# Starting the attention of the first 512 queries after 6 instead of 20 pieces of the in-projection's last part, two pieces per step

## Chip, cores and metric

The kernel runs on one core of one Trainium2 chip. The metric is the device time of one execution in microseconds (us). Three runs of the kernel before gave a median of 2692.12 us (2691.47 to 2698.45).

## The reference

One layer of a hybrid encoder block on 2048 frames of width 1024, in f32. The part that matters here is the stick-breaking attention, 8 heads of width 64, in blocks of 128 queries, strictly causal:

```
z = einsum('bhqd,bhkd->bhqk', qb, kb) * d**-0.5
mask = s_pos[None, :] < t_pos[:, None]
log_one_minus = where(mask, log_sigmoid(-z), 0.0)
between = cumsum(shifted log_one_minus, reverse)      # over later keys
weights = where(mask, exp(log_sigmoid(z) + between), 0.0)
out = einsum('bhqk,bhkd->bhqd', weights, vb)
```

Ahead of it stand the modulated RMSNorm and one in-projection, `proj = h @ w_in`, whose columns are q, k and v of the attention and the inputs of a gated linear attention (GLA). Behind it stand the out-projection, a second norm, the up-projection with a causal convolution and a gate, the down-projection, and a final norm.

## The kernel before

Every f32 matmul against weights is done as three matmuls of rounded parts (high by high, high by low, low by high). The 2048 frames are worked in four chunks of 512, numbered 0 to 3. The in-projection goes over the weight blocks in an order fixed by hand, and stores q, k and v of each chunk in HBM (`q_hi`, `q_lo`, `k_hl`, `v_hl`). In its second half the GLA of the last chunks runs between the matmuls. It ends with the GLA's last tile: four transposes (L467), the split into `mh` and `ml` on ScalarE and VectorE (L470), and their stores `mg_hi` and `mg_lo` (L473) on SyncE's queue (SP).

What then is left of the in-projection is written as a generator, `last_pieces` (L771): v of chunk 3 in four row tiles (L779 to L781, weights against `hh` and `hl`) and the last two heads of k of chunk 3 (L789 to L791). It yields after each **piece**, three matmuls of 128x128 by 512 columns; there are 4 x 8 + 8 = 40 pieces. A finished row tile is split by ScalarE and VectorE into `vt`, of which there is one buffer (L783, L784), and stored (L785).

The attention is a loop of **steps** (L1097): step n takes 128 queries against 512 keys of one head. Its parts are `score` (L981, L982 and on the diagonal the mask, L984), `weigh` (two sigmoids on ScalarE, L1000 and L1001; a scan on VectorE, L1006; a product on GpSimd, L1008), six steps later `turned` (PE transposes, L70, and the split into `ah` and `al`, L129 and L130), and two more steps later `value` (L1033, L1034). Four steps are a unit: one head, one chunk of queries, one chunk of keys. The first 512 queries are steps 0 to 31, and within a unit the widths are 128, 256, 384 and 512 keys. `fetch` (L958) issues the loads of a unit on SP: q (L964), `kt` (L967) and `vt` (L969), six steps ahead; the first two units' are issued before the loop.

The order of PE's matmuls inside the loop is the order in which they are written (`in_order`, L1096). Other engines' instructions and SP's loads are put in an order by a scheduler when the program is built, and each engine and SP then works through its own queue strictly in order. The pieces are woven into the loop by a credit:

```
work, rate, credit, tail = last_pieces(), FR, 0.0, []
for _ in range(PRE):
    next(work)
for u in range((FA + 3) // 4):
    fetch(u)
...
    for n in range(last_step):
        ...
        credit += rate
        while credit >= 1.0:
            credit -= 1.0
            if work is not None and next(work, True):
                work = None
```

`PRE` pieces run before step 0, and `FR` pieces at the end of each step until none is left; the step after that opens the pools of the out-projection (L1102) and begins to load its weights, 1 MB at every sixth step (L1106, `wo`). Whatever the two numbers are, the out-projection of the first chunk is woven in from step 63 on (L1128, L1131). Steps without pieces or out-projection are called **unfilled** here.

Of the kernel before, what the change touches and what calls it, by code (L numbers as in the profile page):

```python
# [32 lines left out]
LATE = 2  # L33
GROUPS = ((0,),(1,),(2,3),(4,5),(6,7))
CUTS = (0,4,8)
PRE = 20
WI = 6
ST = 24
FR = 1.0
FA = 6  # L40
ADA = ((2,2,2,2,1,1,1,1,1,0,1),(1,1,1,1,1,1,0,0,0,0,0))
PREP = ((0,0,0,0,1,0,1,0,1,0,1),(1,0,1,0,1,1,0,0,0,0,0))
# [5 lines left out]
def hybrid_block(ctx, tc, x, c, w_ada, b_ada, g1, w_in, w_fg2, b_fg2, g_gla, w_out, g2,  # L48
# [722 lines left out]
    def last_pieces():  # L771

        hh, hl = hs[3]
        for tt in range(4):
            sl = slice(tt * P, (tt + 1) * P)
            ps = ps_mm.tile([P, CH], F, name="mm")
            for k in range(KD):
                wh, wl = w_v[k]
                pe.matmul(out=ps, lhsT=hh[:, k, sl], rhs=wh, start=k == 0, stop=False)  # L779
                pe.matmul(out=ps, lhsT=hh[:, k, sl], rhs=wl, start=False, stop=False)  # L780
                pe.matmul(out=ps, lhsT=hl[:, k, sl], rhs=wh, start=False, stop=k == KD - 1)  # L781
                yield
            vt = ev.tile([P, H, 2, HD], R, name="vt", bufs=1)  # L783
            split_from_psum(vt[:, :, 0, :], vt[:, :, 1, :], ps.rearrange("p (h d) -> p h d", h=H))  # L784
            dma.dma_start(out=v_hl[3][tt * P:(tt + 1) * P], in_=f32(vt.rearrange("p h a d -> p h (a d)")))  # L785
        ps = ps_mm.tile([P, CH], F, name="mm")
        for k in range(KD):
            wh, wl = w_k[k]
            pe.matmul(out=ps, lhsT=wh, rhs=hh[:, k], start=k == 0, stop=False)  # L789
            pe.matmul(out=ps, lhsT=wh, rhs=hl[:, k], start=False, stop=False)  # L790
            pe.matmul(out=ps, lhsT=wl, rhs=hh[:, k], start=False, stop=k == KD - 1)  # L791
            yield
        eh = ev_tile("eh", R)
        el = ev_tile("el", R)
        split_from_psum(eh, el, ps)
        for a in range(2):
            dma.dma_start(out=k_hl[3][6 + a, 0:64, :], in_=f32(eh[a * 64:(a + 1) * 64]))
            dma.dma_start(out=k_hl[3][6 + a, 64:128, :], in_=f32(el[a * 64:(a + 1) * 64]))
# [289 lines left out]
    last_step = N + LEAD + LATE  # L1088
    work, rate, credit, tail = last_pieces(), FR, 0.0, []
    open_at, start = None, -1  # L1090
    for _ in range(PRE):
        next(work)
# [545 lines left out]
```

## Time and profile before

| | us |
|---|---|
| median of three runs | 2692.12 |
| the profiled execution, its own time | 2685.92 |
| its span, first to last instruction | 2684.2 |
| PE busy (94% of the span) | 2521.2 |
| VectorE busy (68%) | 1831.4 |
| ScalarE busy (49%) | 1306.4 |
| GpSimd busy (48%) | 1289.3 |
| mean granted clock of PE, share of full speed | 0.987 |

Engines: PE is TensorE, PEld its weight loads, DVE VectorE, ACT ScalarE, POOL GpSimd, SPq SyncE's DMA queue. A row of a timeline gives start, duration, engine, line, operation, output<-input and shapes; brackets at its end hold the idle time of the engine just before it and what ended that. Successive matmuls overlap: one of 512 columns is listed with 0.39 us, but the next one starts 0.23 us later. A row of windows gives the stretch, its length, the busy time of PE, PEld, DVE, ACT and POOL (instructions in brackets), the granted PE clock (1.00 is 2.4 GHz, 0.50 is 1.2 GHz), the mean busy share of the 16 DMA engines, and GB/s. A row of waits gives the waiting instruction, its releaser, the total, how often, and the longest. A row of DMA issues gives the count, the size and the time from issue to landing.

### The profile page before, as it was taken

The page shows a single profiled execution, that of the slowest core. Times are in us where ns is not written, and L with a number is a line of the kernel's source. Part 1 is how long each engine was busy: PE and PEld are TensorE (multiplying, and loading weights), DVE is VectorE, ACT ScalarE, POOL GpSimd, SP SyncE. Part 2 cuts the span into 40 slices and gives each one's busy share as a digit, 9 for nine tenths or more (in the row PEclk, how much of TensorE's full clock was granted, in tenths as well). Part 3 has the DMA queues.
Part 4 walks back from the last instruction along what each step waited for, and adds up shares of the span by engine and source line. Part 5 has one row for each costly group of instructions (what it writes and reads, how often), then busy time and mean ns, then how long its engine had stood idle before and what let it go on. Part 6 is the DMA issues. An engine that isn't in the chain of part 4 may idle for free. (4 is left out here: it accounts for less than half of the span.)

```text
span 2684.2 us, 36445 instructions
## 1 busy us (share of the span) xinstructions
PE 2521.2 (94%) x12118; PEld 2060.4 (77%) x12118; DVE 1831.4 (68%) x2511; ACT 1306.4 (49%) x2328; POOL 1289.3 (48%) x1094
## 2 busy tenths in 40 slices
PE   5999999999899999999889999989999999999996
PEld 5788788888677777777777777767877877888885
DVE  6535652254988999998567767788777777454668
ACT  4523234233877888887444444454444444333343
POOL 2202131121755556766655645576566563252446
PEclk9999999999999999999999999999999999999998
DMA  8657954586865444554633443455445447544572
GB/s 284 193 170 253 288 169 144 154 250 183 260 184 172 131 140 146 165 161 131 220 114 114 138 138 102 132 186 169 147 137 173 146 146 252 166 142 128 167 271 79
DMA packets 406827, 459.06 MB, mean 171 GB/s; under 512 B 35806, under 2 KB 271596, under 8 KB 404592
## 3 DMA queue, kind: packets, MB, share of 16 engines
q1 hardware_dynamic: 406640, 456.74, 53.9%
q8 instruction: 96, 1.57, 0.2%
q14 instruction: 91, 0.75, 0.1%
HBM read 313.51 MB, written 143.13 MB: 170 GB/s over the span
## 5 line engine op out<-in xcount | busy, mean ns | idle before, releaser
L1008 POOL TENSOR_TENSOR bt<-bt,om 128x512 f32<-128x512 f32 (+2 forms) x320 | 314.5, 988 | 220.3 <-DVE om L1006 122.9
L1185 POOL TENSOR_TENSOR wub<-ring,wub 128x512 fp32r<-128x512 f32 x176 | 236.5, 1356 | 264.8 <-ACT wub L1184 264.4
L1231 PE MATMUL v<-h,wua 128*128 128x512 f32 x1056 | 259.7, 395 | 7.8 <-DVE halo L1297 5.4
L1231 PE MATMUL v<-h,wub 128*128 128x512 f32 x1056 | 250.2, 393 | 12.5 <-DVE v L1235 6.5
L1231 PE MATMUL g<-h,wub 128*128 128x512 f32 x1056 | 257.9, 390 | 1.5 <-DVE g L1235 1.5
L1006 DVE TENSOR_TENSOR_SCAN om<-sg,om,zero 128x513 f32<-128x513 f32 x189 | 240.6, 1273 | 16.0 <-ACT sg L1000 14.8
L1231 PEld LDWEIGHTS v<-h,wub 128*128 128x128 f32 x1056 | 199.8, 190 | 56.4 <-ACT wub L1184 6.4
L1231 PEld LDWEIGHTS v<-h,wua 128*128 128x128 f32 x1056 | 199.1, 189 | 55.4 <-ACT wua L1184 5.4
L1185 POOL TENSOR_TENSOR wua<-ring,wua 128x512 fp32r<-128x512 f32 x132 | 195.1, 1481 | 77.7 <-ACT wua L1184 73.3
L1231 PEld LDWEIGHTS g<-h,wub 128*128 128x128 f32 x1056 | 198.2, 188 | 43.7 <-DVE g L1235 1.9
L1180 DVE TENSOR_TENSOR ring<-ring 128x512 f32<-128x512 f32 x176 | 172.5, 999 | 85.4 <-DMA ring<-in_w_up_dram 61.7
L1604 PE MATMUL d<-h,wub 128*128 128x512 f32 x924 | 222.9, 391 | 0.0
L70 PE MATMUL tr<-ident,bt 128*128 128x128 f32 x1120 | 179.9, 277 | 37.5 <-DVE al L130 25.0
L1362 POOL TENSOR_TENSOR h<-h,h 128x512 fp32r<-128x512 f32 x77 | 116.6, 1518 | 193.0 <-ACT h L1361 176.5
L130 DVE TENSOR_TENSOR al<-tr,ah 128x512 fp32r<-128x512 f32 (+1 forms) x320 | 193.0, 603 | 19.5 <-ACT ah L129 18.7
L1604 PEld LDWEIGHTS d<-h,wub 128*128 128x128 f32 x924 | 173.5, 188 | 37.6
L286 POOL TENSOR_TENSOR wr<-wst,wr 128x1024 fp32r<-128x1024 f32 x28 | 69.4, 2484 | 276.2 <-ACT wr L285 276.2
L129 ACT ACTIVATE ah<-tr 128x512 fp32r<-128x512 f32 (+1 forms) x320 | 179.4, 561 | 25.9 <-PE tr L70 25.3
L70 PEld LDWEIGHTS tr<-ident,bt 128*128 128x128 f32 x1120 | 126.6, 140 | 84.6 <-DVE al L130 35.8
L1001 ACT ACTIVATE bt<-z 128x512 f32<-128x512 f32 (+2 forms) x320 | 173.6, 543 | 0.0
L1184 ACT ACTIVATE wub<-ring 128x512 fp32r<-128x512 f32 x176 | 107.8, 625 | 134.4 <-DVE ring L1180 83.9
L400 PE MATMUL mm<-wr,hh 128*128 128x512 f32 (+1 forms) x448 | 169.5, 378 | 2.9 <-DVE vt L130 2.2
(309 smaller groups left out, 6067.6 us busy)
## 6 DMA issues: line engine op xcount, KB each, us to landing
ring<-in_w_up_dram SPq DMA_DIRECT2D x176, 256.0 KB, 3.9
ring<-hid_s SPq DMA_DIRECT2D x154, 256.0 KB, 4.1
wst<-in_w_in_dram SPq DMA_DIRECT2D x45, 512.0 KB, 7.6
hid_s<-cval SPq DMA_DIRECT2D x88, 256.0 KB, 2.3
kt<-k_hl SPq DMA_DIRECT2D x80, 256.0 KB, 3.0
vt<-v_hl SPq DMA_DIRECT2D x80, 256.0 KB, 3.3
hid_s<-ring SPq DMA_DIRECT2D x66, 256.0 KB, 2.7
ast<-in_w_ada_dram SPq DMA_DIRECT2D x32, 512.0 KB, 5.5
```

The source lines that it names most:

```text
L70: pe.transpose(out=o, in_=i, identity=ident)
L129: act.activation(out=hi, in_=ps, func=AF.Copy)
L130: dve.tensor_tensor(out=lo, in0=ps, in1=f32(hi), op=ALU.subtract)
L400: pe.matmul(out=ps[:, :n], lhsT=hh[:, k, sl], rhs=wh, start=k == 0, stop=False)
L1001: act.activation(out=b1, in_=z[:, :w], func=AF.Sigmoid, scale=0.125)
L1006: dve.tensor_tensor_scan(out=om[:, 0:n_][:, ::-1], data0=beta[:, 0:n_][:, ::-1], data1=zero[0][:, 0:1].broadcast_to([P, n_]), initial=firs ...
L1008: pool.tensor_tensor(out=b1, in0=b1, in1=om[:, 1:w + 1], op=ALU.mult)
L1180: dve.tensor_tensor(out=t_, in0=a, in1=b, op=op)
L1185: eng.tensor_tensor(out=t_[:, 1], in0=src, in1=f32(t_[:, 0]), op=ALU.subtract)
L1231: pe.matmul(out=ps, lhsT=lhsT, rhs=rhs, start=begin and k == 0 and m == 0, stop=k == KH - 1 and m == 2, skip_group_check=not begin)
L1362: pin(eng.tensor_tensor(out=t_[:, 1], in0=src, in1=f32(t_[:, 0]), op=ALU.subtract))
L1604: pin(pe.matmul(out=ps, lhsT=hd[:, l_, tsl], rhs=w[:, r_], start=begin and q == 0 and m == 0, stop=q == NQ2 - 1 and m == 2, skip_group_che ...
```

## The change

Two constants are changed: the loop begins after 6 pieces, and each step takes two pieces instead of one.

```
-PRE = 20
+PRE = 6
 WI = 6
 ST = 24
-FR = 1.0
+FR = 2.0
```

PE's order ahead of step 0. `tp` transposes belong to the GLA's last tile, `mm` matmuls to pieces, and `z` is a step's score. Before, the end of the 20 pieces:

```order
L779 MATMUL mm<-wr,hh 128x512
L780 MATMUL mm<-wr,hh 128x512
L781 MATMUL mm<-wr,hl 128x512
L981 MATMUL z<-kt,qh 128x256
L982 MATMUL z<-kt,ql 128x256
L984 LDWEIGHTS identb
L984 MATMUL z<-mask,identb 128x128
L779 MATMUL mm<-wr,hh 128x512
```

In the change, from the GLA's last transposes on:

```order
L70 MATMUL tp<-ident,sq 128x128 x4
L779 MATMUL mm<-wr,hh 128x512
L780 MATMUL mm<-wr,hh 128x512
L781 MATMUL mm<-wr,hl 128x512
L779 MATMUL mm<-wr,hh 128x512
L780 MATMUL mm<-wr,hh 128x512
L781 MATMUL mm<-wr,hl 128x512
L981 MATMUL z<-kt,qh 128x256
L982 MATMUL z<-kt,ql 128x256
L984 LDWEIGHTS identb
L984 MATMUL z<-mask,identb 128x128
L779 MATMUL mm<-wr,hh 128x512
```

Up to the sixth piece PE's order is the same in both; the first score has moved ahead of the 14 pieces that stood before it.

SP's queue at the same place (`mg_hi` and `mg_lo` are the GLA's last stores, the first `kt` and `vt` are unit 0's, `v_hl_75<-vt` stores a row tile of the pieces):

```order
 L967 DMA kt<-k_hl_68 128x512
 L969 DMA vt<-v_hl_72 128x4x128
-L785 DMA v_hl_75<-vt 128x1024
 L967 DMA kt<-k_hl_68 128x512
 L969 DMA vt<-v_hl_72 128x4x128
```

The first row here is directly behind the store of `mg_lo` in both programs; a row tile's store has moved from between the loads of units 0 and 1 to a place behind the first loads of `kt` and `vt`.

PE's order where the pieces end, in the change, from the last piece (step 16) into step 18 (`tr` are the attention's transposes, `av` its values):

```order
L789 MATMUL mm<-hh,wr 128x512
L790 MATMUL mm<-hl,wr 128x512
L791 MATMUL mm<-hh,wr 128x512
L981 MATMUL z<-kt,qh 128x256
L982 MATMUL z<-kt,ql 128x256
L984 LDWEIGHTS identb
L984 MATMUL z<-mask,identb 128x128
L70 MATMUL tr<-ident,bt 128x128 x2
L1033 MATMUL av<-ah,vt 128x384
L1034 MATMUL av<-al,vt 128x384
L981 MATMUL z<-kt,qh 128x384
L982 MATMUL z<-kt,ql 128x384
```

Steps 17, 18 and 19 have one piece each before and none in the change.

## Rows read from the trace of the kernel before

**Rows 1.** The page, its first part: busy time of each engine
```profile
PE 2521.2 (94%) x12118; PEld 2060.4 (77%) x12118; DVE 1831.4 (68%) x2511; ACT 1306.4 (49%) x2328; POOL 1289.3 (48%) x1094
```

**Rows 2.** Windows: busy time of each engine before, in and after the unfilled stretch
```profile
core 0: us, PE busy (x) PEld busy (x) DVE busy (x) ACT busy (x) POOL busy (x), PEclk, DMA share, GB/s
650.83:691.38 40.55, 40.39 (x228) 32.77 (x226) 27.80 (x61) 24.91 (x62) 18.13 (x24) 1.00 0.68 209
691.38:757.00 65.62, 52.39 (x322) 39.52 (x321) 65.21 (x120) 58.72 (x138) 48.49 (x51) 1.00 0.99 295
780.00:800.00 20.00, 20.00 (x112) 16.58 (x111) 14.42 (x25) 12.78 (x28) 10.40 (x12) 1.00 0.53 163
```

**Rows 3.** Waits of PE from 691 to 757 us (total, times, longest)
```profile
PE tr L70 <- DVE al L130: 8.3, 16, 1.2
```

**Rows 4.** Timeline of PE around step 0
```profile
650.60 0.39 PE L781 MATMUL mm<-wr,hl 128*128 128x512 f32 x1
650.83 0.39 PE L779 MATMUL mm<-wr,hh 128*128 128x512 f32 x1
...
660.35 0.28 PE L981 MATMUL z<-kt,qh 128*128 128x256 f32 x1
```

**Rows 5.** Timeline of SP's queue: the loads that step 0 needs, a later load
```profile
650.98 0.36 SPq L473 DMA_DIRECT2D mg_lo<-ml  x1
651.44 0.49 SPq L967 DMA_DIRECT2D kt<-k_hl  x1
653.73 0.36 SPq L969 DMA_DIRECT2D vt<-v_hl  x1
...
700.43 0.58 SPq L967 DMA_DIRECT2D kt<-k_hl  x1
```

**Rows 6.** Timeline of PE: the score that waited for the later load
```profile
703.62 0.36 PE L981 MATMUL z<-kt,qh 128*128 128x256 f32 x1 [0.59 <-DMA kt<-k_hl]
```

**Rows 7.** Windows: DMA traffic after the first load
```profile
654.00:654.25 0.25, 0.25 (x3) 0.20 (x2) 0.00 (x0) 0.00 (x0) 0.00 (x0) 1.00 0.22 74
654.25:654.50 0.25, 0.25 (x3) 0.21 (x2) 0.00 (x0) 0.00 (x0) 0.00 (x0) 1.00 0.00 0
```

**Rows 8.** DMA issues from 654.6 to 654.9 us: the second load
```profile
kt<-k_hl SPq DMA_DIRECT2D x1, 256.0 KB, 5.0
```

**Rows 9.** Timeline of PE: gaps elsewhere in the kernel
```profile
111.13 0.48 PE L70 MATMUL tp<-ident,gfr 128*65 128x128 f32 x1 [2.41 <-DVE gfr L521]
...
383.33 0.30 PE L70 MATMUL tp<-ident,xt 128*128 128x128 f32 x1 [4.26 <-DVE ms L123]
...
1361.56 0.47 PE L1231 MATMUL v<-h,wub 128*128 128x512 f32 x1 [2.41 <-DVE v L1235]
...
1808.52 7.92 PE L1231 MATMUL v<-h,wub 128*128 128x512 f32 x22 [6.01 <-ACT wub L1184]
```

**Rows 10.** Windows: the granted clock behind those gaps
```profile
111.00:116.00 5.00, 4.87 (x15) 3.91 (x16) 4.96 (x4) 0.00 (x0) 2.21 (x1) 0.66 0.14 24
383.00:389.00 6.00, 5.67 (x34) 5.70 (x35) 2.15 (x8) 3.52 (x8) 1.66 (x3) 0.72 0.69 240
1361.00:1364.00 3.00, 2.44 (x11) 2.04 (x12) 2.04 (x4) 1.75 (x3) 2.92 (x3) 1.00 0.47 135
1808.52:1815.00 6.48, 6.48 (x17) 5.09 (x18) 6.48 (x7) 1.54 (x3) 3.55 (x4) 0.56 0.21 78
```

**Rows 11.** Timeline of PE: first instruction of steps 17, 20, 21, 24 and 25
```profile
686.20 0.28 PE L981 MATMUL z<-kt,qh 128*128 128x256 f32 x1
...
691.38 0.28 PE L981 MATMUL z<-kt,qh 128*128 128x256 f32 x1
...
692.38 0.28 PE L981 MATMUL z<-kt,qh 128*128 128x256 f32 x1
...
696.73 0.28 PE L981 MATMUL z<-kt,qh 128*128 128x256 f32 x1
...
697.96 0.28 PE L981 MATMUL z<-kt,qh 128*128 128x256 f32 x1
```
## The prediction

> **What bounds the kernel now.** The page comes first: PE is busy for 94% of the span and no other engine for more than 68% [rows 1]. So the question is where PE idles, and whether the change makes it idle more or less. I then took the windows around the pieces [rows 2]. From 650.83 us, behind the sixth piece, to 691.38, the start of step 20 and so the end of the pieces, PE is busy for 40.39 of 40.55 us: PE is the limit there, and DVE has 40.55 - 27.80 = 12.75 us to spare. From 691.38 to 757 the steps are unfilled; there DVE is busy for 65.21 of 65.62 us, PE for only 52.39, and the waits name DVE's split as what PE's transposes wait for [rows 3]. DVE is the limit of that stretch, which ends when the out-projection comes in. From 780 to 800 PE is full again, 20.00 of 20 us, so that time lost before is not won back there [rows 2].
>
> The timeline shows what step 0 needs. PE runs piece after piece up to 660.35, when step 0's score follows without a gap [rows 4]. The keys of that step are loaded on SP right behind the GLA's last stores: `mg_lo` at 650.98, `kt` at 651.44 [rows 5]. Before, nine microseconds of pieces cover that load. The sixth piece ends at 650.83 [rows 4], before the load is even issued.
>
> **The change, part by part.** The work is the same: as many pieces, steps, loads and stores. Three things move.
>
> First, step 0's score now stands where the seventh piece starts, at 650.83, and PE works in order, so that every later piece waits with it. SP's order up to the `kt` load is the same, and nothing ahead of it on PE has moved, so I keep its issue at 651.44. The nearest row for issue to use is the one `kt` load that PE waited for: issued at 700.43, used at 703.62, 3.19 us [rows 5, 6]. That puts step 0 at 651.44 + 3.19 = 654.63, a stall of 3.8 us. It is bounded from below by the DMA traffic, which is still going on after 654.00 and is nought from 654.25 on [rows 7]: some 3.3 us. From above by the next `kt` load, which took 5.0 us to land in denser traffic [rows 8]: 651.44 + 5.0 - 650.83 = 5.6 us. I take 3.8, since in the quiet slice the load must have been done. ScalarE, DVE and GpSimd do nothing useful for the attention in that time; the table load of ScalarE and the setting of constants fall into it and cost nothing.
>
> Second, the clock. A PE that has been idle for some time comes back at the lower of its two levels. Behind the gap of 4.26 us the clock averages 0.72 over 6 us: 6 x 0.28 = 1.7 us lost by a PE that works without pause. Behind one gap of 2.41 us it averages 0.66 over 5 us, again 1.7 us. Behind another gap of 2.41 us it stays at 1.00. Behind the gap of 6.01 us it averages 0.56 over 6.48 us, 2.85 us lost [rows 9, 10]. My stall of 3.8 us is nearest to the gap of 4.26, so I take 1.7 us; the ends are nothing and 2.85. The Trainium skill, TensorE: Matmul & The Clock Gate, section "Why this matters for your kernels", warns against idle gaps between bursts of matmuls in mid-kernel, as one of them brings the lower clock back. By that rule the term stands; by the gap of 2.41 us that left the clock alone it would be nought and the whole sum 5.3 us. The trace bears the rule out for both long gaps, and for one of the two short ones.
>
> Third, the cover. One piece takes (660.35 - 650.83)/14 = 0.68 us of PE [rows 4]. Steps 17, 18 and 19 had a piece each, and take 691.38 - 686.20 = 5.18 us, of which the attention's own matmuls are 5.18 - 3 x 0.68 = 3.14 us [rows 11]. In the change the pieces have been done earlier, with two to a step, and these three steps are unfilled. What unfilled steps of the same three widths take is to be seen at steps 21 to 23, 692.38 to 696.73, 4.35 us, and at steps 25 to 27, 697.96 to 703.62, 5.66 us [rows 6, 11], the latter with 0.59 us of a late load in it. So the cover that is lost costs between 4.35 - 3.14 = 1.2 and 5.66 - 3.14 = 2.5 us; below that nothing, if DVE has no arrears and PE can run on ahead. I take 1.5: the steps with two pieces leave DVE more spare time than those with one, so it enters the unfilled stretch without arrears.
>
> What I cost at nothing: the row tiles' stores on SP, now behind the loads of `kt` and `vt` for units 1 and 2. The single `vt` buffer is free again when the store has landed, and the next tile is ready four steps and eight pieces (8 x 0.68 = 5.4 us, and the scores besides) later; PE has a second accumulator in the meantime. If that cover is gone, ScalarE stands with step 5's sigmoids behind the split, and two steps' scores are the reserve. The loads of units 1 and 2 are issued within a few microseconds of the first one and are wanted at steps 4 and 8, which come later than unit 0 by at least as many pieces as before, so they hide. The out-projection's weights begin to load three steps earlier by number, but still behind the end of the pieces; they are wanted from step 63 on. The moves of DVE's and ScalarE's instructions follow PE's order and keep each behind what it needs.
>
> The sum is 3.8 + 1.7 + 1.5 = 7.0 us on the profiled execution, which took 2685.92 us (a span of 2684.2 and 1.7 outside): 2692.9. The median of the runs is 6.2 us above that execution, so for a median I add the 7.0 to 2692.12: 2699.1 us. A measurement of this kernel tells a change from no change at about 0.3%, which is 8.1 us, or 2684.0 and 2700.2. The forecast lies just inside: slower by 0.26%.
>
> **The rivals.**
>
> A stall without a fall of the clock: 3.8 + 1.5 = 5.3 us, 2697.4. For it speaks the gap of 2.41 us that left the clock at 1.00; against it three gaps out of four. 0.24.
>
> A longer stall that ends on the slower side. If the first `kt` takes as long as the second (5.0 us), PE idles for 5.6 us, nearly as long as in the gap of 6.01 us, behind which 2.85 us were lost. Then 5.6 + 2.85 + 1.5 = 10.0 us, 2702.1. It decides at a landing after some 656 us. For it: the first load shares the DMA engines with the GLA's stores, which are in flight. Against it: the same traffic in the trace is over by 654.25. 0.24.
>
> The change does not move the point at which the attention waits: if the keys are there in time after all (a scheduler can order SP's queue, and the GLA's tail can end earlier), only the lost cover is left, 1.5 us, 2693.6. Against it: SP's order in the program is the same up to that load, and it stands behind stores that wait for the GLA's last transposes. 0.08.
>
> A gain. The stretch from 650.83 to 691.38 is PE's, the one behind it DVE's, and DVE idles for 12.75 us in the first. If the attention of the second can be drawn into the first, DVE ends earlier: step 0 at 654.63 instead of 660.35 is worth up to 5.7 us, 2686.4, if DVE then paces every step; without the stall it would be 9.5 us. This decides at whether a step with two pieces is shorter than DVE's part of it: with 2 x 0.68 and 3.14/3 us of matmuls it is 2.4 us, against the 4.35/3 = 1.5 that an unfilled step takes. It is longer, so PE paces these steps, and DVE's spare time only moves. The Trainium skill, Perfetto Trace Analysis, section "Optimization Strategy", says that where the most contended engine changes over time, interleaving the regimes may help. The trace has the two regimes, but this interleaving packs the first one's work more densely instead of stretching it over the second. 0.06.
>
> **How the numbers follow.** The forecast has 0.38, and the rivals in their order 0.24, 0.24, 0.08 and 0.06. Slower by over 0.3% are four fifths of the long stall (0.19), a quarter of the forecast (0.10), which lies 1.1 us from the bound, and 0.01 of the rest: 0.30. Faster by over 0.3% is a third of the gain: 0.02. Within 0.3%: 0.68. The range reaches from just under the case without a stall, 2692.5, to the sum of all three upper ends, 5.6 + 2.85 + 2.5 = 11.0 us, 2703.1, and a little of the spread of the runs: 2704.0. It leaves out the gain and the far ends of the others.
>
> **What would show it.** In the profile of the changed kernel, PE should stand before step 0's first score for 3 to 4 us, released by the DMA of `kt`, with `kt` issued at the same time against the GLA's last store as before. The granted clock should be at 0.50 for about 3 us around or shortly behind that gap, while the pieces' matmuls start about twice as far apart. From then on PE should be full until the start of step 17, with about 2.4 us to a step, and DVE with more spare time than now. The first unfilled step should be 17, and the stretch of unfilled steps three steps longer, with DVE its limit. It would be wrong if PE passes step 0 without a wait, if the clock stays at 1.00, if steps 17 to 19 take no longer than their matmuls, or if PE waits for `ah` and `al`, for `vt`'s buffer or for a later load within the filled steps.

## The result, and the profile after

The changed kernel took 2706.49 us (median; 2698.79 to 2718.97) beside 2691.47 us (2686.07 to 2698.45) for the kernel before: a ratio of 1.0063 with a 95% interval of 1.0048 to 1.0079, 13 to 21 us slower. On a second occasion it was 1.0044 (1.0027 to 1.0062). The forecast of 2699.1 us had the sign, but the time lies above its range, which ended at 2704.0.

The profiled execution took 2706.49 us, its span is 2704.8 us against 2684.2, and the granted clock 0.983 against 0.987. PE is busy for 8.8 us more with as many instructions [rows 1], so part of the 20.6 us is slower matmuls; the other 11.8 us are idle time of PE:

```profile
PE 2530.0 (94%) x12118; PEld 2065.7 (76%) x12118; DVE 1835.2 (68%) x2511; ACT 1305.6 (48%) x2328; POOL 1282.2 (47%) x1094
```

The GLA's last store, `mg_lo`, is issued at 652.45 us, 1.47 us later than before [rows 5]; in the profiles of the other runs it comes between 646.17 and 653.34, so I don't put this down to the change, and count from there on. The timeline of PE of the changed kernel, the first matmul of steps 0, 20, 24, 28, 32, 40 and 63:

```profile
656.13 0.55 PE L981 MATMUL z<-kt,qh 128*128 128x256 f32 x1 [3.67 <-DMA kt<-k_hl]
...
699.16 0.28 PE L981 MATMUL z<-kt,qh 128*128 128x256 f32 x1
...
708.23 0.35 PE L981 MATMUL z<-kt,qh 128*128 128x256 f32 x1 [2.42 <-DMA qh<-q_hi]
...
718.58 0.55 PE L981 MATMUL z<-kt,qh 128*128 128x256 f32 x1 [3.77 <-DMA qh<-q_hi]
...
726.29 0.35 PE L981 MATMUL z<-kt,qh 128*128 128x256 f32 x1 [0.53 <-DMA qh<-q_hi]
...
742.44 0.41 PE L981 MATMUL z<-kt,qh 128*128 128x256 f32 x1
...
777.78 0.40 PE L981 MATMUL z<-kt,qh 128*128 128x512 f32 x1
```

Step 0 stands 3.67 us for `kt`, as forecast. But steps 24, 28 and 32 stand too, for `qh`, which PE waits for nowhere in this stretch of the kernel before. Windows of the changed kernel: the stall, the steps up to 4, steps 20 to 40 in all, and of these steps 20 to 36 and 36 to 40:

```profile
652.45:656.13 3.68, 0.01 (x1) 0.03 (x1) 0.00 (x0) 0.55 (x1) 0.00 (x0) 0.92 0.76 214
656.13:666.43 10.30, 10.30 (x37) 8.04 (x38) 3.31 (x8) 3.62 (x9) 1.91 (x3) 0.70 0.76 236
...
699.16:742.44 43.28, 28.08 (x153) 21.78 (x152) 34.23 (x65) 28.27 (x69) 25.46 (x27) 0.86 0.98 259
...
699.16:731.51 32.35, 22.17 (x127) 17.72 (x125) 25.50 (x54) 21.09 (x55) 14.53 (x21) 0.84 0.95 253
731.51:742.44 10.93, 5.90 (x29) 4.06 (x28) 8.72 (x12) 7.18 (x16) 10.93 (x7) 0.93 1.06 276
```

The same stretch in the kernel before, steps 20 to 40, and of these steps 20 to 36:

```profile
691.38:722.83 31.45, 23.84 (x152) 18.18 (x151) 31.29 (x61) 28.06 (x69) 24.61 (x25) 1.00 0.96 288
...
691.38:715.43 24.05, 18.62 (x125) 14.79 (x124) 23.89 (x52) 21.36 (x55) 17.21 (x20) 1.00 0.92 293
```

There DVE works for 31.29 of 31.45 us; now for 34.23 of 43.28. It is no longer the limit, PE waits, and PE's clock falls to 0.86 on the mean. Counted from `mg_lo`, the change is 6.3 us later at step 20 (46.71 against 40.40), then loses 11.8 us up to step 40 and wins 1.4 back by step 63: 16.7 us. Of the span's 20.6 us, 1.5 lie ahead of this and 2.4 behind. The 11.8 us are of two kinds: steps 20 to 36 take 8.3 us longer (32.35 against 24.05), and there PE waits for q (1.4 of it are left when the loads are moved, as e5 shows below); steps 36 to 40 take 3.5 us longer (10.93 against 7.40), and there PE waits 3.0 us not for data, but for one long product of GpSimd (L1008), which the last section shows.

The waits of PE from 690 to 780 us in the changed kernel (total, times, longest):

```profile
PE tr L70 <- DVE al L130: 6.7, 13, 0.9
PE z L981 <- DMA qh<-q_hi: 6.7, 3, 3.8
PE tr L70 <- POOL bt L1008: 3.0, 1, 3.0
PE z L982 <- DMA ql<-q_lo: 1.7, 3, 0.7
```

Why q is late is to be seen on SP. There are two q buffers (`qp`, L930), so unit 6, which begins with step 24, can load its q only when unit 4's last score, step 19, is done. SP's queue in the kernel before, where step 19 starts at 689.58:

```profile
690.00 1.09 SPq L964 DMA_DIRECT2D qh<-q_hi  x2
691.18 1.19 SPq L964 DMA_DIRECT2D ql<-q_lo  x2
692.46 0.54 SPq L839 DMA_DIRECT2D wo<-wo_s  x1
693.11 0.46 SPq L797 DMA_DIRECT2D k_hl<-eh  x1
```

And in the changed kernel, where step 19 starts at 698.00:

```profile
696.17 0.45 SPq L839 DMA_DIRECT2D wo<-wo_s  x1
696.85 1.10 SPq L797 DMA_DIRECT2D k_hl<-eh  x2
698.04 2.98 SPq L798 DMA_DIRECT2D k_hl<-el  x2
701.12 1.32 SPq L964 DMA_DIRECT2D qh<-q_hi  x2
702.53 4.13 SPq L964 DMA_DIRECT2D ql<-q_lo  x2
...
707.81 0.50 SPq L839 DMA_DIRECT2D wo<-wo_s  x1
708.41 1.09 SPq L964 DMA_DIRECT2D qh<-q_hi  x2
```

Before, q is issued 0.4 us after step 19's score has started, ahead of the first 1 MB load of the out-projection's weights and of the last pieces' stores. In the change those stand ahead of it: it comes 3.1 us after the score, and its four transfers take until 706.66 to issue instead of 2.4 us. SP's own waits, from 690 to 745 us, name the large load for that:

```profile
SPq L964 <- DMA wo<-wo_s: 3.1, 1, 3.1
```

In the kernel before SP has such waits too (4.4 us in two, from 684 to 738 us), but the q of unit 6 has gone out ahead of them.

Unit 7's q, at 708.41, stands behind the second 1 MB load; before, unit 7's q went ahead of the second one.

### The profile page after: what moved, and what is told of

It reads as the page before. It is cut to its first block, busy times and chain, and to the rows that moved or that the text cites. A ratio compares the mean times of both kernels' runs of the same rounds, so it can differ in the third digit from the quotient of the medians.

```text
span 2704.8 us, 36446 instructions
## 1 busy us (share of the span) xinstructions
PE 2530.0 (94%) x12118; PEld 2065.7 (76%) x12118; DVE 1835.2 (68%) x2511; ACT 1305.6 (48%) x2328; POOL 1282.2 (47%) x1094
## 5 line engine op out<-in xcount | busy, mean ns | idle before, releaser
L1008 POOL TENSOR_TENSOR bt<-bt,om 128x512 f32<-128x512 f32 (+2 forms) x320 | 310.9, 975 | 233.5 <-DVE om L1006 134.9
```

What stands on the lines that cost most here:

```text
L1008: pool.tensor_tensor(out=b1, in0=b1, in1=om[:, 1:w + 1], op=ALU.mult)
```

## The experiments

Theory A: two costs that add, the stall at step 0 with its clock, and 1 MB loads on SP ahead of q. Rival B: the unfilled steps of the first 512 queries want more data than arrives, whatever else is loaded. Rival C: it is chance of phase, any 1 MB load on a step at which a unit is fetched.

The table gives for each run the start of steps 0, 20 and 63 in its profile, counted from its `mg_lo` store, the difference at step 63 to the kernel before, and the measured ratio of whole times to runs of the kernel before on the same chip. The steps are the sharper measure: behind step 63, where nearly all the kernels do the same work in the same order of steps, the profiles differ among themselves (1924.6 us in the kernel before, 1938.5 us in e4). But each row is one profile: the two of the change are 4.5 us apart at step 63, those of e5 and e12, one kernel too, 0.8.

| run | step 0 | 20 | 63 | at 63 | ratio (95%) |
|---|---|---|---|---|---|
| before | 9.37 | 40.40 | 108.63 | | |
| the change | 3.68 | 46.71 | 125.33 | +16.7 | 1.0063 (1.0048 to 1.0079) |
| e11, the change again | 3.72 | 46.42 | 120.78 | +12.2 | 1.0044 (1.0027 to 1.0062) |
| e1: opened at 21 | 3.68 | 46.62 | 123.20 | +14.6 | 1.0033 (1.0021 to 1.0045) |
| e2: 12 pieces, opened at 18 | 3.92 | 39.83 | 117.61 | +9.0 | 1.0037 (1.0024 to 1.0049) |
| e3: 12 pieces, opened at 21 | 3.92 | 39.83 | 113.35 | +4.7 | 1.0015 (1.0001 to 1.0029) |
| e4: before, opened at 22 | 9.37 | 40.39 | 109.71 | +1.1 | 1.0019 (1.0001 to 1.0037) |
| e5: the change, loads from 32 | 3.69 | 45.17 | 115.80 | +7.2 | 1.0029 (1.0010 to 1.0048) |
| e12: e5 again | 3.67 | 45.38 | 115.05 | +6.4 | 1.0022 (1.0008 to 1.0036) |
| e6: 12 pieces, loads from 32 | 3.93 | 39.84 | 109.49 | +0.9 | 1.0005 (0.9992 to 1.0019) |
| e10: the change, third q buffer | 3.77 | 46.66 | 119.00 | +10.4 | 1.0082 (1.0053 to 1.0111) |
| e8: 6 pieces, one a step | 3.75 | 37.16 | 109.63 | +1.0 | 1.0007 (0.9992 to 1.0021) |
| e14: 20 pieces, two a step | 9.37 | 44.03 | 119.62 | +11.0 | 1.0058 (1.0039 to 1.0076) |
| e7: 13 pieces, one a step | 4.61 | 37.05 | 106.28 | -2.4 | 1.0009 (0.9992 to 1.0026) |
| e13b: the same, loads from 32 | 4.60 | 36.23 | 107.97 | -0.7 | 0.9997 (0.9983 to 1.0010) |
| e13: 12 pieces, 0.8 a step | 3.93 | 37.39 | 112.22 | +3.6 | 1.0011 (0.9998 to 1.0023) |

All edits are to the changed kernel; "opened" is the step at which the out-projection's pools open and the 1 MB loads begin (L1102).

**Four runs: with and without the stall, opened early or late.** e1:

```
-            if work is None and open_at is None:
+            if work is None and open_at is None and n >= 21:
```

> The change as it is (6 pieces ahead of step 0, two to a step), but the out-projection's pools open at step 21 as before, not at 18, so that its 1 MB loads stand on SP's queue at the steps at which they stood. Theory A (two costs that add: about 6.3 us by the stall at step 0 and the clock behind it, about 10 us by the loads of 1 MB that now stand ahead of the loads of q): only the first is left, +6 to +8 us against the kernel before; PE stands 3.7 us before step 0's score, and its waits for q from step 20 on, 8.4 us in the changed kernel, are under 2 us. Rival B (the three more unfilled steps themselves are what makes q late): the full +15 us, with the waits for q. Rival C (any load of 1 MB that falls on a step at which a unit is fetched): as A here.

e2 and e3 have this with 18 and with 21, and

```
-PRE = 6
+PRE = 12
...
-FR = 2.0
+FR = 1.65
```

> 12 pieces ahead of step 0 and 1.65 a step, so that the pieces end at step 16 and the pools open at step 18, as in the change, but step 0 has the cover of six more pieces. Theory A: no stall of over 0.5 us at step 0 and no clock fall there, but PE's waits for q behind step 20 (5 to 9 us) as in the change: +8 to +11 us against the kernel before. Rival B: the same +8 to +11. If the late loads were a consequence of the stall, it would be 0 to +2 us.

> As the last one, but with the pools opened at step 21. Neither stall nor early loads; what is left is three more unfilled steps. Theory A: the lost cover alone, 0 to +2 us, no waits for q over 2 us. Rival B: +8 to +11 us, as with the pools opened at 18.

e4 is the kernel before (`PRE = 20`, `FR = 1.0`) with `n >= 22`.

> The kernel before (20 pieces, one a step) with the pools opened one step later, at 22 instead of 21, so that the 1 MB loads fall on steps 22, 28, 34 and every second of them on a step at which a unit is fetched, as 18 and 30 do in the change (before it is 21, 27, 33, none of them on one). Rival C (the coincidence is what counts): +5 to +10 us against the kernel before, with PE waiting for q or kt at steps 24 to 36. Theory A (that the loads stand earlier against the attention's is what counts) and rival B: within 2 us of the kernel before.

The stall stands by itself: with 12 pieces step 0 does not wait, and step 20 comes 6.9 us earlier than in the change (39.83 against 46.71). And the loss behind step 20 does not come from the stall: without it, in e2, steps 20 to 63 still take 77.78 us, against 68.23 before and 78.62 in the change. e4 (+1.1 us at step 63; its whole time, up to +0.37%, is not explained by this stage) does not test C on SP: its first 1 MB load, at 694.37, stands behind the q of the unit fetched at that step, at 691.24. What speaks against C is e1, and e14 below: their loads begin at steps 21 and 11, so that none falls on a step at which a unit is fetched, and PE waits for q in both. Between A and B these runs do not decide, since the edit of e1 and e3 did not do what it says. SP's order is made by the scheduler, and with the pools opened at 21 it put the first 1 MB load ahead of unit 6's q all the same. SP's queue of e3:

```profile
683.54 0.45 SPq L839 DMA_DIRECT2D wo<-wo_s  x1
685.25 2.20 SPq L797 DMA_DIRECT2D k_hl<-eh  x2
687.54 1.39 SPq L798 DMA_DIRECT2D k_hl<-el  x2
689.02 2.28 SPq L964 DMA_DIRECT2D qh<-q_hi  x2
```

e1's waits for `qh` are 5.2 us, e3's for `kt` 2.5: misses against A as I had put it. The loads had to be moved further.

**Loads moved out, a third buffer, and the other direction.** e5 (e6 the same with `PRE = 12`, `FR = 1.65`):

```
-WI = 6
+WI = 4
...
-            if work is None and open_at is None:
+            if work is None and open_at is None and n >= 32:
```

> The change as it is, but the 1 MB loads of the out-projection's weights begin at step 32 (one at every fourth step), behind the whole of the first 512 queries. In the traces of the four runs so far the first of these loads stood on SP ahead of the q of the sixth unit (counted from 0) whenever the pieces ended at step 16, even where the pools opened at 21; so those runs did not take it away. Theory A' (these loads, ahead of q on SP and in the same DMA traffic, make q late): PE's waits for q between steps 20 and 32 fall from 8.4 us to under 2, steps 20 to 63 take at most 72 us against 78.6 in the change and 68.2 before, and the kernel is +6 to +10 us against the one before. Rival B (unfilled steps of the first 512 queries want more loads a microsecond than arrive, with or without the weights): the waits for q stay at 5 us or more, steps 20 to 63 take 76 us or more, +13 us or more.

> 12 pieces ahead of step 0 and 1.65 a step, so that there is no stall and the pieces end at step 16, and the 1 MB loads begin at step 32 as in the last one. Theory A': what is left is the lost cover of three steps, 0 to +3 us against the kernel before, with steps 20 to 63 at 69 to 71 us. Rival B: +5 us or more, with PE waiting for q or kt between steps 20 and 32.

e5's longest waits of PE, from 649 to 767 us, and its windows of steps 0 to 4, 20 to 40 and, of these, 20 to 36:

```profile
PE tr L70 <- DVE al L130: 9.7, 19, 1.2
PE z L981 <- DMA kt<-k_hl: 3.7, 1, 3.7
PE tr L70 <- DVE om L1003: 2.4, 3, 1.0
```

```profile
654.06:662.81 8.75, 8.75 (x37) 6.89 (x38) 3.30 (x8) 3.56 (x9) 1.92 (x3) 0.83 0.90 278
...
695.54:728.43 32.89, 24.02 (x154) 18.25 (x152) 32.73 (x63) 28.48 (x69) 24.17 (x26) 1.00 0.99 278
...
695.54:721.01 25.47, 18.82 (x127) 14.85 (x125) 25.31 (x54) 21.76 (x55) 16.75 (x21) 1.00 0.97 266
```

No wait for q is left, and from step 20 to 40 DVE is busy for 32.73 of 32.89 us: the limit that the forecast had. B falls: these steps are as unfilled as in the change, the DMA engines are as busy (0.99 of the time against 0.98), and nothing is late. The rest of e5's 7.2 us is the stall with its clock and the lost cover, and e6, without the stall, has 0.9 us.

In the change two things stood ahead of unit 6's q, a 1 MB load and the stores of the last pieces. In e5 the stores still do; its step 19 starts at 694.38:

```profile
693.22 1.11 SPq L797 DMA_DIRECT2D k_hl<-eh  x2
694.42 1.43 SPq L798 DMA_DIRECT2D k_hl<-el  x2
695.95 1.19 SPq L964 DMA_DIRECT2D qh<-q_hi  x2
```

q comes 1.6 us behind the score instead of 3.1, its four transfers are issued in 2.5 us instead of 5.5, and PE does not wait. So the stores alone don't make q late.

e10:

```
-    qp = sb(st, "qp", 2, "right")
+    qp = sb(st, "qp", 3, "right")
...
-            for sl in (slice(0, CH // 2), slice(CH // 2, CH)):
-                tiles = [tq.tile([P, CH // 2], F, name=f"tq{i}") for i in range(4)]
+            for sl in (slice(i * P, (i + 1) * P) for i in range(4)):
+                tiles = [tq.tile([P, P], F, name=f"tq{i}") for i in range(4)]
```

> The change as it is, with three q buffers instead of two (and the early sums, from step 208 on, in quarter tiles instead of halves to make room, which may cost or give a few us far behind the stage). With two buffers a unit's q can be loaded only when the last score two units before is done, four steps ahead; with three it is issued at the fetch, ahead of the first 1 MB load. Theory A': PE's waits for q between steps 20 and 36 fall from 8.4 us to under 3, and steps 20 to 63 take 70 to 74 us instead of 78.6. Rival B: the loads are short of bandwidth, so that the wait only goes over to kt or vt, and the steps take 76 us or more.

Here the 1 MB loads begin at step 18 as in the change, but unit 6's q is issued at 692.32, before the first of them (695.90). The window of steps 20 to 40, and the one late load that came behind it, at step 44:

```profile
699.91:733.35 33.44, 24.17 (x154) 18.25 (x152) 33.28 (x63) 29.02 (x70) 24.71 (x26) 1.00 0.98 274
```

```profile
742.93 0.47 PE L981 MATMUL z<-kt,qh 128*128 128x512 f32 x1 [3.08 <-DMA kt<-k_hl]
```

DVE is the limit again, 33.28 of 33.44 us, with the same loads at the same steps. So it is q's place behind the large loads, with only two buffers to issue it ahead, that makes it late, and not the amount of data. Steps 20 to 36 take 25.46 us, as in e5, instead of 32.35. GpSimd's long product is gone as well, and steps 36 to 40 take 7.98 us instead of 10.93. The Trainium skill, Perfetto Trace Analysis, section "Optimization Strategy", says that gaps that repeat on the engine that should be full can mean that there is no room for the next tile; this run agrees, three waits of 6.7 us in all have gone with one more buffer. Part of it came back as the `kt` wait above. The whole time is not better: behind step 63 the profile is 13 us longer than before's, which the smaller tiles of the early sums may be the cause of; that was not tried apart, and e4, without them, is as long there.

e7:

```
-PRE = 6
-WI = 6
+PRE = 13
+WI = 5
...
-FR = 2.0
+FR = 1.0
...
-            if work is None and open_at is None:
+            if work is None and open_at is None and n >= 27:
```

> The other direction: 13 pieces ahead of step 0 and one a step, so that step 0 has its cover (seven pieces, 4.8 us, behind the load of kt) and the pieces reach up to step 26 instead of 19; the pools open at 27 with a 1 MB load at every fifth step. If the unfilled steps of the first 512 queries are where time is lost, and filling seven more of them takes PE's gaps there away (4.5 us of gaps in steps 20 to 28 of the kernel before): -2 to -5 us against the kernel before. If DVE paces the whole loop, or the 1 MB loads, now five steps apart, only come late elsewhere: -1 to +3 us.

In the steps the gain is there, 2.4 us at step 63. In whole time it does not show.

**The halves of the change, and a version between.** e8 has `FR = 1.0` and `WI = 4`, e14 only `PRE = 20`, and e13 `PRE = 12`, `FR = 0.8`, `WI = 4`.

> One half of the change alone: 6 pieces ahead of step 0, but one a step, so that the pieces reach up to step 33; the pools open at 34 with a 1 MB load at every fourth step (at every sixth the last would come too late for the out-projection). Theory A': the stall at step 0 with its clock fall, 5 to 7 us, stays; the loads of 1 MB stand behind the first 512 queries, so that PE waits for q under 1 us; and the fourteen more filled steps take PE's gaps there away, as they did with 13 pieces, where the start of step 63 lay 2.4 us earlier after the last of the GLA's stores than before. Step 63 at -1 to +4 us against the kernel before. If the late loads belonged to the early start itself, it would be +10 us or more.

> The other half alone: 20 pieces ahead of step 0, then two a step, so that there is no stall, the pieces end at step 9, and the pools open at 11 with a 1 MB load at every sixth step. Theory A': steps 10 to 31 are all unfilled and run with the 1 MB loads beside them, eleven steps of the kernel before lose their cover (0.9 us for three: 3 to 4 us for ten), and q comes late as in the change, in more units: +10 to +20 us against the kernel before, with PE's waits for q, kt and vt over 8 us and the clock falling behind them. If what the change lost came from its stall, this one is within 0 to +4 us.

> A version that may beat both: 12 pieces ahead of step 0 (cover enough, no stall) and 0.8 a step, so that the pieces reach up to step 34; the pools open at 35, a 1 MB load at every fourth step. A step then has 1.05 + 0.8 x 0.68 = 1.6 us of PE, near the 1.5 us at which an unfilled step of the first 512 queries runs. If PE's and DVE's work can be laid side by side here, step 63 starts 3 to 6 us earlier than in the kernel before (13 pieces and one a step: 2.4 us), and the whole kernel is -2 to -6 us. If DVE paces it all, or the 1 MB loads make later q and kt late, 0 +- 2 us.

The early start alone can't be told from no change: the 3.7 us of stall are there, and yet step 63 comes only 1.0 us later. That the fourteen more covered steps win the rest back is not shown apart. Two pieces a step alone cost +0.39% to +0.76%. In e14's profile step 32 waits 3.66 us for `qh`, and steps 20 to 40 take 37.61 us with DVE busy for 33.31. Its waits named for data come to 5.1 us, fewer than the 8 expected; another 2.0 us, at step 28, are put down to ScalarE. e13 is a miss: it is not faster. Its window of four steps with 0.8 of a piece each, steps 24 to 28:

```profile
696.59:703.39 6.80, 6.48 (x42) 5.33 (x41) 6.74 (x14) 6.44 (x18) 3.54 (x5) 1.00 0.75 246
```

DVE is busy for 6.74 of 6.80 us and has become the limit, so thinning the pieces out hardly shortens a step: with one piece a step, four steps took 6.87 us before (684.51 to 691.38), with PE full and DVE busy for 5.87. And behind the pieces, steps 36 to 44 take 18.29 us against 14.31 in the kernel before, with the 1 MB loads now all there. The Trainium skill's advice to interleave regimes (Perfetto Trace Analysis, "Optimization Strategy") gains nothing more here that the runs show.

**The change and its mended form side by side, and e7 with the loads from 32.** e11 is the change, e12 is e5, e13b is e7 with `WI = 4` and `n >= 32`.

> The change itself once more, beside the next kernel on the same chip: +14 to +18 us against the kernel before, with PE's waits for q between steps 20 and 36 at 7 us or more in the profiled run, and the stall of 3.7 us at step 0.

> The change with the 1 MB loads from step 32 on, one at every fourth step, once more. If the loads on SP ahead of q are the cause of the larger part: +5 to +9 us against the kernel before, 7 to 11 us faster than the change on the same chip. If they only move a wait about: within 4 us of the change.

> 13 pieces ahead of step 0, one a step, and the 1 MB loads from step 32 on, one at every fourth step: step 0 covered, pieces up to step 26, no large load within the first 512 queries. By the table of steps of the version with the loads from step 27 on, step 63 starts 2 to 4 us earlier than in the kernel before; whole time -3 to +1 us, a gain that the runs may not be able to tell. If it is +3 us or more, the earlier start costs something that the stage does not show.

The change was 1.0044 (+11.8 us, less than the expected 14 to 18), the same with the loads moved 1.0022 (+5.9 us): moving the loads gives 5.9 us back in whole time, less than the 7 to 11 expected and just over the 4 that I had set as the other theory's bound. The intervals against the kernel before overlap, 1.0027 to 1.0062 and 1.0008 to 1.0036. Set against each other, the six runs of e11 have a mean of 2698.6 us and the twelve of e12 2693.7, 4.9 us apart, with a 95% interval of 1.5 to 8.4: that there is a gain is clear, its size only roughly. In e11's profile PE's waits for data are a miss against the 7 us expected: 3.7 us, of which 2.4 at step 28 are put down to a load of `vt`, which the score does not read; unit 7's `qh`, which it does read, is issued at 702.04, behind the second 1 MB load at 701.44. Its waits of PE from 690 to 780 us, other than for DVE's split, and its windows of steps 20 to 36 and 36 to 40:

```profile
PE tr L70 <- POOL bt L1008: 3.0, 1, 3.0
PE z L981 <- DMA vt<-v_hl: 2.4, 1, 2.4
PE z L982 <- DMA ql<-q_lo: 1.3, 3, 0.5
```

```profile
696.06:723.39 27.33, 20.32 (x126) 16.24 (x125) 25.10 (x54) 21.46 (x55) 15.75 (x21) 0.94 0.95 290
723.39:734.80 11.41, 6.41 (x30) 4.50 (x29) 8.73 (x12) 6.89 (x15) 11.41 (x7) 0.82 0.97 266
```

Steps 20 to 63 take 74.36 us in e11 and 69.67 in e12, 4.7 us apart; in the first profiles of the two kernels it was 78.62 and 70.63, 8.0 apart. Where the loss lies differs: in steps 20 to 36, where q is late, the first profile of the change loses 6.9 us against e5, e11 only 1.9 against e12 (25.47 us in both); in steps 36 to 40, behind GpSimd's product, 3.5 and 4.0 (7.42 in both). So on the second occasion the late q is the smaller part of what the early loads cost. No version beat the kernel before: e13b is nearest, at 0.9997, and its step 63 comes 0.7 us earlier, not the 2 to 4 expected.

## Why the prediction was wrong

**The stall: right.** Forecast 3.8 us with `kt` issued 0.46 us behind `mg_lo` and used 3.19 us later; measured 3.67 us, issued at 652.91, 0.46 behind, used 3.22 later. The other profiles that begin after 6 pieces have 3.66 to 3.75.

**The clock: right in kind, too small in size.** Forecast 1.7 us, with ends at nothing and 2.85, and the clock at 0.50 for about 3 us. Over steps 0 to 4 the change has 0.70 for 10.30 us, 3.1 us lost, more than the upper end, with about 6 us at 0.50; e5, with the same gap, 0.83 for 8.75 us, 1.5 lost. That is the difference at step 20 between the two, 46.71 and 45.17. All seven profiles with the gap show the fall, five of them the longer one.

**The lost cover: right in size, not in place.** Forecast 1.5 us, in steps 17 to 19. These cost nothing: from step 17 to 20 the change takes 3.14 us, the matmuls alone, which the prediction had named as a sign of being wrong. Its reason, that DVE has no arrears there, spoke for its lower end of nothing. The cost comes behind: steps 20 to 36 take 25.47 us in e5, e6 and e12, 1.4 us more than the 24.05 before, with DVE busy throughout.

With the loads out of the way the forecast's own sum stands: 7.0 us were forecast, and e5 and e12 are 7.2 and 6.4 us late at step 63, +7.8 and +5.9 us in whole time. That it fits so well is in part luck: these two have the shorter fall of the clock, and with the change's own they would be some 1.5 us later.

**The step that failed** is the sentence in what was costed at nothing: "The out-projection's weights begin to load three steps earlier by number, but still behind the end of the pieces; they are wanted from step 63 on." It asks when the moved loads are wanted, and not what they are moved past: on SP they passed the q of unit 6 and of unit 7, and q has no slack, because its buffer comes free only four steps ahead. Four filled steps are 6.87 us; four unfilled ones 5.35 to 6.89 us. The prediction had weighed the loads of units 1 and 2 alone. The views had two warnings: the DMA share of 0.99 in the unfilled stretch [rows 2], of which I used only the busy times, and the load that was already 0.59 us late there [rows 6], which I used as a price and not as a sign that the stretch was at its edge. Between steps 20 and 63 the early loads cost 8.0 us in the first pair of profiles and 4.7 in the second, and 5.9 in whole time on the second occasion. Of this, 6.9 and 1.9 us in steps 20 to 36 are the late q. Another 3.5 and 4.0 us in steps 36 to 40 are PE's wait for GpSimd's long product; it is gone in e5 and e12, where the loads are moved, and in e10, where q is not late, but by which path the early loads bring it about stays open.

**Of the rivals,** the one with a longer stall came nearest in size (10.0 us against 15.0 by the medians), but not by its mechanism: the stall was no longer than forecast, and only its 2.85 us of clock were about right. The gain fell, as argued: two-piece steps take 2.3 us (29.59 for steps 4 to 16), and DVE is busy for 20.45 of these 29.59. The other two fell with the clock and the stall that the profiles show.

Of what was to be seen, "From then on PE should be full until the start of step 17" came true, "with DVE its limit" for the unfilled steps did not. That wait for a later load was named only for the filled steps.

## What to carry to other kernels

When a change moves the step at which something large is loaded, list what it passes in the issuing queue and how far ahead each of those loads can be issued: with a double buffer that is until the last use two tiles before, and this lead, in microseconds, can shrink when the steps lose work. Ask it of the stretch that the work was taken out of, not only of the one that it was put into. And an edit that names a step does not place a load: here the scheduler put a load at the same place for opening at 18 and at 21, so the order itself has to be read. Last, split a loss by steps before putting all of it down to one wait: here 3.5 to 4.0 us of it stood behind another.

## What the runs showed of the hardware that was not expected

The same idle time does not cost the same clock. Behind gaps of 3.66 to 3.75 us at the same place, the granted clock was at 0.50 for some 6 us in five profiles (the change, e1, e8, e10, e11), and for some 3 us in two (e5, e12). Windows of e11, whose step 0 starts at 653.36 (the third number from the end is the granted clock):

```profile
656.00:657.00 1.00, 1.00 (x5) 0.81 (x3) 0.00 (x0) 0.04 (x1) 0.00 (x0) 0.50 0.82 258
...
658.00:659.00 1.00, 1.00 (x4) 0.80 (x3) 0.88 (x3) 0.17 (x1) 0.00 (x0) 0.53 1.16 331
659.00:660.00 1.00, 1.00 (x7) 0.71 (x6) 0.00 (x0) 0.00 (x0) 0.64 (x1) 1.00 1.21 340
```

And of e12, whose step 0 starts at 652.57:

```profile
655.00:656.00 1.00, 1.00 (x4) 0.75 (x3) 0.00 (x0) 0.00 (x0) 0.00 (x0) 0.50 1.04 325
656.00:657.00 1.00, 1.00 (x7) 0.85 (x6) 0.22 (x1) 0.85 (x3) 0.00 (x0) 0.99 0.94 255
```

Why the lower level holds twice as long in the one as in the other was not settled.

GpSimd's product (L1008) of a full 128x512 tile takes about 1.1 us. In one place, between steps 36 and 39, it took 5.5 us in the three profiles whose pools open at 18 with two q buffers (the change, e2, e11), and PE waited 3.0 us for it (steps 36 to 40 take 10.93 and 11.41 us in the change and e11, 7.42 in e5 and e12); in the same steps of all others it took 2.0 us at most. The line's instructions from 728 to 745 us in the change, and from 712 to 727 in the kernel before:

```profile
L1008 POOL TENSOR_TENSOR bt<-bt,om x9: 410/1091/5526, 727.7 to 743.7; 128x512 f32<-128x512 f32 x6, 128x128 f32<-128x128 f32 x1, 128x256 f32<-128x256 f32 x1, 128x384 f32<-128x384 f32 x1
```

```profile
L1008 POOL TENSOR_TENSOR bt<-bt,om x9: 412/1097/2007, 711.6 to 725.7; 128x512 f32<-128x512 f32 x6, 128x128 f32<-128x128 f32 x1, 128x256 f32<-128x256 f32 x1, 128x384 f32<-128x384 f32 x1
```

(The three numbers are the least, the median and the longest in ns.) In the change three of DVE's scans follow each other meanwhile with only a split between; whether that is the cause was not tried.
